# Expert rows weighted at eviction, added to x by accumulating transfers, and a last store that waits for no other

## The chip, the cores and the metric

One core of a Trainium2 chip runs one program. The number that counts is the device time in microseconds (us) of one execution, the median of several. TensorE (PE) multiplies matrices, VectorE (DVE), ScalarE (ACT) and GpSimd (POOL) work element by element. SyncE (SP) issues most transfers, on hardware queue q1; transfers issued by POOL go on software queue q0. All of them are carried out by the same 16 DMA engines.

## The reference

Two transformer blocks in float32 on 512 tokens of 1024 numbers. Only the seam between them matters here: the mixture of experts that ends the first block, and the norms behind it.

```python
def hierarchical_moe(h, ...):                 # 16 experts, 2 of them for each token
    ...                                       # combine[n, e]: the two weights of token n, else 0
    a = jnp.einsum("nd,edf->nef", hf, w_gate)
    b = jnp.einsum("nd,edf->nef", hf, w_up)
    u = jax.nn.silu(a) * b * combine.astype(hf.dtype)[..., None]
    return jnp.einsum("nef,efd->nd", u, w_down)
...
x = x + hierarchical_moe(rmsnorm(x, norm_moe_g), ...)   # end of the first block
x = rmsnorm(x, norm_final_g)
h = rms_norm(x, norm_mix_g_2); proj = h @ w_in_2        # start of the second block
```

## The kernel before

Tokens lie in four tiles of 128 rows, `k.x[:, t, :]`, 128x1024 float32 each (512 KB). Matrices are split into a high and a low part (`wh`, `wl`: ACT makes the first, DVE the second, lines 126 and 127), and a product is three matmuls (lines 112 to 114).

**Experts** (`moe`). `Route` sorts the tokens by expert into blocks of 128 slots. Every expert e fetches its rows of h from DRAM by an indirect transfer (`gather`, line 1350), multiplies them (`up`, `act`, `turn`, `down`), evicts the result from PSUM to a tile `ey` by ACT (line 1393) and puts the rows by an indirect transfer from POOL (line 1394) to the DRAM tensor `y_d`: row n for a token's first choice, row 512+n for its second, so no row is written twice. Slots without a token write nothing. Each of the 16 stores waits for the one ahead to land, because all of them write `y_d`. A loop for experts with over 128 tokens stands behind a branch (`tc.If(n > 0)`); with these inputs it is skipped.

**Seam** (`mixer2`). Instructions are written in a fixed order for PE, ACT, DVE, POOL and SP (`manual_schedule`), and every engine takes its own in that order. For each token tile t: `Combine.load` fetches the two halves of `y_d` (`yg`, SP, line 1588); `add0` and `add1` add them to x, each times a column of weights `wt` (DVE, line 1599); `gained` computes the sum of squares of x on ACT (line 1608) and z = x times the final gain on DVE (line 1609), `squares` that of z on ACT (1613); `stats` makes both norms' factors (three small DVE operations and a power on POOL, line 186); `norm` scales z (DVE, line 1628); `turn` transposes it on PE (line 218), and `lo` writes the low part (DVE, line 224). Then `k.head` multiplies with three weight tiles (`hraw`, loaded by SP, split at once by `split_w`). PE is kept busy meanwhile by `values(n)`: n of 16 steps of another product, V of the second block's cross-attention (line 608). `kv.load_v` loads its weights.

Where the loads stand on SP: the three weight tiles, the four `yg` of tiles 0 and 1, two loads for `values`, the four `yg` of tiles 2 and 3.

Of the kernel before, what the change touches and what calls it, by code (L numbers as in the profile page):

```python
# [10 lines left out]
FT = mybir.dt.float32  # L11
# [3 lines left out]
OP = mybir.AluOpType  # L15
# [1127 lines left out]
class Route:  # L1143
# [2 lines left out]

    def __init__(self, k, pool, lg, out):
        self.k, self.pool, self.lg, self.out = k, pool, lg, out  # L1150
# [59 lines left out]
    def place(self, O):  # L1210
# [33 lines left out]
        G = t(S24, "G")  # L1244
# [53 lines left out]
    def weights(self):  # L1298

        nc, t, v = self.k.nc, self.t, self.k.nc.vector  # L1300
        S4 = [P, NT, 4]
        eg = t(S4, "eg")
        v.tensor_tensor(eg, self.gl, self.gm.unsqueeze(2).to_broadcast(S4), op=OP.subtract)
        nc.scalar.activation(eg, eg, AF.Exp)
        e2 = t([P, NT], "e2")
        v.tensor_tensor(e2, self.m2, self.m1, op=OP.subtract)
        nc.scalar.activation(e2, e2, AF.Exp)
        pg = t([P, NT], "pg")
        v.tensor_reduce(pg, eg, axis=AX.X, op=OP.add)
        v.reciprocal(pg, pg)  # L1310
        wt = self.out.tile([P, 2, NT], FT, name="wt")
# [4 lines left out]
        return wt  # L1316


class Expert:
# [3 lines left out]

    def __init__(self, k, pool, hg, ids, h_d, y_d, weights):
        self.k, self.pool, self.hg, self.ids = k, pool, hg, ids
        self.h_d, self.y_d, self.weights = h_d, y_d, weights

    @staticmethod  # L1330
# [54 lines left out]
    def down(self):  # L1385
        k, nc = self.k, self.k.nc
        y = self.pool.tile([P, D], FT, name="ey")
        for c in range(2):
            w = next(self.weights)
            py = k.ps_mm.tile([P, T], FT, name="mm")  # L1390
            for i in range(2):
                k.mm3(py, self.uT[:, i, :], w[:, i, :], i == 0, i == 1)
            nc.scalar.activation(y[:, c * 512 : (c + 1) * 512], py, AF.Copy)
        nc.gpsimd.indirect_dma_start(
            out=self.y_d[:, :], out_offset=bass.IndirectOffsetOnAxis(ap=self.ids[1], axis=0),
            in_=y, in_offset=None, bounds_check=2 * T - 1, oob_is_err=False,
        )
# [9 lines left out]
        yield from Expert.down_list(k, dw[e])  # L1407


def moe(k, mst, rp, hg_pool, pools, src, w_prev, kv, vraws, early, lists):  # L1410
# [6 lines left out]
    rt = Route(k, rtp, lg, rp)  # L1417
# [77 lines left out]
    with ExitStack() as est:  # L1495
# [7 lines left out]
        with k.tc.manual_schedule(engines={*MANUAL, E.Pool}):  # L1503
            rt.choose()
            keys(3)
            rt.count()
            rt.place(ep.tile([P, D], FT, name="ey").rearrange("p (a b) -> p a b", a=8))
            keys(4)
            ids = rt.table()
            ex = [  # L1510
                Expert(
                    k, ep, hgs[e % 2], [ids[:, i, e : e + 1] for i in range(2)], h_d, y_d, weights
                )
                for e in range(NE)
            ]
            for x in ex[:2]:
                x.gather()
            xi = rt.extra()
            wt = rt.weights()
            weights.fill(2)  # L1520
            for _ in kjob:
                pass
            ex[0].rows()
            weights.fill(AHEAD)
            ex[1].rows()
            ex[2].gather()
# [17 lines left out]
        with k.tc.manual_schedule(engines={*MANUAL, E.Pool}):  # L1544
# [2 lines left out]
            kv.load_v(0, 4, vraws[0])  # L1547
            x.down()
            kv.load_v(4, 6, vraws[1])
        with k.tc.If(n > 0):  # L1550
            with k.tc.For_i(0, n) as b:
                e = nc.values_load(xi[0:1, bass.ds(b, 1)], min_val=0, max_val=NE - 1)
                idb = [ep.tile([P, 1], I32, name=f"idb{i}") for i in range(2)]
                for i in range(2):
                    nc.vector.tensor_copy(idb[i], ids[:, i, bass.ds(b + NE, 1)])
                wg, wu, wd = [w[bass.ds(e, 1)].rearrange("a r c -> (a r) c") for w in ws]
# [4 lines left out]
                x = Expert(k, ep, hgs[0], idb, h_d, y_d, weights)  # L1561
                x.gather()
                x.rows()
                for h in range(2):
# [1 line left out]
                x.act()  # L1566
                x.turn()
                x.down()
    return y_d, wt


class Combine:
# [4 lines left out]


    def __init__(self, k, pool, t):
        self.k, self.pool, self.t = k, pool, t  # L1580
        self.xs = k.x[:, t, :]

    def load(self, y_d):
        self.ys = []
        for c in range(2):
            y = self.pool.tile([P, D], FT, name="yg", bufs=2 * NT)
            r0 = c * T + self.t * P
            self.k.nc.sync.dma_start(y, y_d[r0 : r0 + P, :])
            self.ys.append(y)

    def add0(self, wt):
        self.add(0, wt)

    def add1(self, wt):
        self.add(1, wt)

    def add(self, c, wt):
        w = wt[:, c, self.t : self.t + 1]
        self.k.nc.vector.scalar_tensor_tensor(
            self.xs, self.ys[c], w, self.xs, op0=OP.mult, op1=OP.add  # L1600
        )

    def gained(self, gf):

        nc = self.k.nc
        self.hn, self.z = self.ys
# [26 lines left out]
        self.k.nc.scalar.activation(self.xs, self.z, AF.Copy, scale=self.r[:, 0:1])  # L1633


def mixer2(k, y_d, wt, kv, vraws, vdone):
# [4 lines left out]
    with ExitStack() as st:  # L1641
# [3 lines left out]
        with k.sb("m2n", bufs=1, side="right") as np_:  # L1645
# [11 lines left out]
            with k.tc.manual_schedule(engines={*MANUAL, E.Pool, E.SP}):  # L1657
# [3 lines left out]
                for g, n in ((gf, "norm_final_g"), (gm, "norm_mix_g_2")):  # L1661
                    ap = inp[n] if len(inp[n].shape) == 1 else inp[n].rearrange("a d -> (a d)")
                    nc.sync.dma_start(g, ap.partition_broadcast(P))
                hvs = []
                for c in (CQ, CK, CQ + P):
                    hvs.append(
                        k.load_raw([(None, wj[:, :, c : c + P])], KD, P, [(np_, 3)], "hraw")
                    )
                for c in cs[:2]:
                    c.load(y_d)  # L1670
                kv.load_v(6, 8, vraws[0])
                for c in cs[2:]:
                    c.load(y_d)

                def turn(t):
                    turns = k.turn_job(hT, cs[t].hn, t)
# [8 lines left out]
                    cs[t].gained(gf)  # L1685
                    cs[t].squares()

                hws = [k.split_w(v, [(np_, 3)]) for v in hvs]
                values(5)
                cs[0].add0(wt)  # L1690
                cs[0].add1(wt)
                gained(0)
                values(5)
                cs[1].add0(wt)
                cs[1].add1(wt)
                cs[0].stats()
                gained(1)
# [5 lines left out]
                cs[2].add1(wt)  # L1703
                values(2)
                lo(t0)
                cs[1].norm(gm)
                gained(2)
                values(2)
                t1 = turn(1)
                cs[3].add0(wt)  # L1710
                cs[2].stats()
                cs[3].add1(wt)
                lo(t1)
                cs[2].norm(gm)
                gained(3)
                cs[3].stats()
                cs[3].norm(gm)

# [268 lines left out]
def build(ctx, tc, inp, out):  # L1987
# [25 lines left out]
    with k.sb("m2T", bufs=1) as m2T:  # L2013
# [22 lines left out]
        with k.sb("x1kv", bufs=1) as pool:  # L2036
# [6 lines left out]
        with k.sb("moer", bufs=1) as rp:  # L2043
            kv = MemoryKV(k, k.mT2, inp["w_k_xa_2"][0], inp["w_v_xa_2"][0])
            vraws = [raws[i] for i in "pb"]
            with ExitStack() as mst:
                y_d, wt = moe(
                    k, mst, rp, lambda: (ost.close(), right(pst, "moehg", bufs=1))[1],
                    [raws[i] for i in "pqb"], oT, k.mview(inp["xa_wo"][0]), kv, vraws, early,
                    lists,  # L2050
                )
            pst.close()
            mg, gst = mixer2(k, y_d, wt, kv, vraws, bst.close)
    xst = ExitStack()

    def out2():
# [40 lines left out]
```

## Time and profile before

| | us |
|---|---|
| median of 3 runs (1672.4 to 1673.55) | 1672.48 |
| the profiled execution's own time | 1674.39 |
| its span, first to last instruction | 1672.7 |
| PE busy in the span | 1620.5 (97%) |
| DVE / ACT / POOL busy | 970.6 / 711.6 / 260.1 |

Busy times of engines overlap. The time around the span is 1.69 us. Differences are worked out in the span and then put on the median.

### The profile page before, as it was taken

What the parts mean: (1) busy time and instruction counts of PE and PEld (TensorE: products, weight loads), DVE (VectorE), ACT (ScalarE), POOL (GpSimd) and SP (SyncE); (2) the same over time, 40 slices, a digit from 0 to 9 for tenths busy, and PEclk for the clock granted to TensorE, in tenths of its full rate; (3) what the DMA queues carried; (4) which work ended last, traced back from release to release, by engine and by line L of the source; (5) the groups of instructions that cost most, each with busy time, mean ns of one, the idle gap of its engine ahead of it and who ended that gap; (6) DMA issues with size and microseconds to landing.
All of it is one profiled execution on the core that took longest, in us unless ns stands there. A gap on an engine that the chain in (4) does not pass through costs nothing.

```text
span 1672.7 us, 20550 instructions
## 1 busy us (share of the span) xinstructions
PE 1620.5 (97%) x7710; PEld 1319.2 (79%) x7710; DVE 970.6 (58%) x1494; ACT 711.6 (43%) x1136; POOL 260.1 (16%) x262
## 2 busy tenths in 40 slices
PE   7998999999999999899999999999999999999998
PEld 6866888788787886588877888888888888888886
DVE  5679997666558996748876333345545333333223
ACT  4254554344428996646644322234434222222212
POOL 3399000300012331102210011110000000000000
PEclk9999999999999999999999999999999999999999
DMA  6332323457469998742233333344123233333231
GB/s 189 90 94 65 89 82 104 161 151 227 141 197 305 316 326 293 251 124 73 67 106 102 89 94 95 95 151 126 51 76 94 75 97 89 100 89 112 90 98 53
DMA packets 253762, 218.65 MB, mean 131 GB/s; under 512 B 13871, under 2 KB 216111, under 8 KB 253660
## 3 DMA queue, kind: packets, MB, share of 16 engines
q1 hardware_dynamic: 247180, 205.51, 40.4%
q0 software_dynamic: 4608, 8.40, 1.4%
q10 hardware_dynamic: 1872, 3.41, 0.5%
q8 instruction: 61, 1.00, 0.2%
q14 instruction: 41, 0.34, 0.1%
HBM read 208.87 MB, written 16.79 MB: 135 GB/s over the span
## 4 chain that ended last, share of the span: by engine, by line
PE 70%; DVE 10%; DMA 9%; issue 6%; ACT 2%; POOL 2%; SPq 0%; POOLq 0%; DVEq 0%; ACTq 0%
PE mm L112 21%; PE mm L114 21%; PE mm L113 21%; DMA y_d<-ey,ids 7%; DVE wl L127 2%; PE mm L583 1%; DVE hn L630 1%; DVE acc L952 1%; DMA wraw<-in_w_in_dram 1%; PE s L112 1%; PE pt L209 1%; PE s L114 1%; PE s L113 1%; DMA hg<-h_d,ids 1%; PE pt L1072 1%
## 5 line engine op out<-in xcount | busy, mean ns | idle before, releaser
L127 DVE TENSOR_TENSOR wl<-wraw,wh 128x1024 fp32r<-128x1024 f32 (+1 forms) x331 | 399.7, 1221 | 362.1 <-ACT wh L126 356.1
L126 ACT ACTIVATE wh<-wraw 128x1024 fp32r<-128x1024 f32 x334 | 340.5, 1028 | 592.7 <-PE mm L113 308.9
L112 PE MATMUL mm<-hT2h,wh 128*128 128x512 f32 (+1 forms) x408 | 156.8, 384 | 0.3 <-ACT hT2h L220 0.3
L113 PE MATMUL mm<-hT2l,wh 128*128 128x512 f32 (+1 forms) x408 | 155.8, 382 | 0.3 <-DVE hT2l L224 0.3
L114 PE MATMUL mm<-hT2h,wl 128*128 128x512 f32 (+1 forms) x408 | 155.8, 382 | 0.0
L112 PE MATMUL mm<-fhTh,wh 128*128 128x512 f32 (+1 forms) x376 | 143.7, 382 | 0.0
L114 PE MATMUL mm<-fhTh,wl 128*128 128x512 f32 (+1 forms) x376 | 143.6, 382 | 0.0
L113 PE MATMUL mm<-fhTl,wh 128*128 128x512 f32 (+1 forms) x376 | 143.6, 382 | 0.0
L112 PE MATMUL mm<-hTh,wh 128*128 128x512 f32 (+1 forms) x280 | 107.9, 385 | 0.0
L113 PE MATMUL mm<-hTl,wh 128*128 128x512 f32 (+1 forms) x280 | 106.7, 381 | 0.1
L114 PE MATMUL mm<-hTh,wl 128*128 128x512 f32 (+1 forms) x280 | 106.6, 381 | 0.0
L114 PEld LDWEIGHTS mm<-hT2h,wl 128*128 128x128 f32 x408 | 76.7, 188 | 16.3
L113 PEld LDWEIGHTS mm<-hT2l,wh 128*128 128x128 f32 x408 | 76.8, 188 | 15.5 <-DVE hT2l L224 0.5
L112 PEld LDWEIGHTS mm<-hT2h,wh 128*128 128x128 f32 x408 | 76.8, 188 | 15.4 <-ACT hT2h L220 0.5
L112 PEld LDWEIGHTS mm<-fhTh,wh 128*128 128x128 f32 x376 | 70.8, 188 | 15.1
L114 PEld LDWEIGHTS mm<-fhTh,wl 128*128 128x128 f32 x376 | 70.8, 188 | 15.1
L113 PEld LDWEIGHTS mm<-fhTl,wh 128*128 128x128 f32 x376 | 70.8, 188 | 15.1
L952 DVE SCALAR_TENSOR_TENSOR acc<-cu,hw,acc 128x511 f32<-128x511 f32 (+14 forms) x90 | 71.9, 799 | 0.9
L113 PE MATMUL mm<-wl,gTh 128*128 128x512 f32 x176 | 69.6, 396 | 0.0
L114 PE MATMUL mm<-wh,gTl 128*128 128x512 f32 x176 | 69.6, 396 | 0.0
L112 PE MATMUL mm<-wh,gTh 128*128 128x512 f32 x176 | 69.6, 395 | 0.0
L1938 DVE TENSOR_TENSOR fu<-fu,mm 128x512 f32<-128x512 f32 x22 | 15.1, 688 | 82.8 <-PE mm L114 82.8
(470 smaller groups left out, 3511.0 us busy)
## 6 DMA issues: line engine op xcount, KB each, us to landing
wraw<-in_w_in_dram SPq DMA_DIRECT2D x92, 512.0 KB
wraw<-in_expert_w_gate_dram SPq DMA_DIRECT2D x64, 256.0 KB
wraw<-in_expert_w_up_dram SPq DMA_DIRECT2D x64, 256.0 KB
wraw<-in_expert_w_down_dram SPq DMA_DIRECT2D x32, 512.0 KB
wraw<-in_w_gate_ffn_dram SPq DMA_DIRECT2D x22, 512.0 KB
wraw<-in_w_up_ffn_dram SPq DMA_DIRECT2D x22, 512.0 KB
wraw<-in_w_down_ffn_dram SPq DMA_DIRECT2D x22, 512.0 KB
wraw<-in_w_out_dram SPq DMA_DIRECT2D x16, 512.0 KB
```

The lines of the kernel that those rows point to most:

```text
L112: nc.tensor.matmul(out, a.hi, b.hi, start=first, stop=False)
L113: nc.tensor.matmul(out, a.hi, b.lo, start=False, stop=False)
L114: return nc.tensor.matmul(out, a.lo, b.hi, start=False, stop=last)
L126: a = nc.scalar.activation(dst.hi, src, AF.Copy)
L127: b = (lo or nc.vector).tensor_tensor(dst.lo, src, hi, op=OP.subtract)
L209: nc.tensor.transpose(pt[:, jj, :], hn[:, half * 4 + jj :: KD], self.ident)
L583: nc.tensor.matmul(ps[:, :M], w[:, j, :], self.mT[:, j, :], start=j == 0, stop=j == KD - 1)
L630: self.k.nc.vector.scalar_tensor_tensor(self.hn[t], self.xs[t], self.r[t][:, 0:1], self.g, op0=OP.mult, op1=OP.mult)
L952: yield nc.vector.scalar_tensor_tensor(acc[:, s:], u[:, :n], w, acc[:, s:], op0=OP.mult, op1=OP.add)
L1072: nc.tensor.transpose(pt[:, kt, :], p[:, kt * P : (kt + 1) * P], k.ident)
L1938: nc.vector.tensor_tensor(u, u, pu, op=OP.mult)
```

## The change

Four parts. (1) `Route.weights` now spreads the weights over the slots (two DVE operations more), a new `row_weights` turns them into one column per expert (8 matmuls, a DVE copy), and ACT applies that column when it evicts (`scale=self.rw[:, 0:1]`). (2) In `Combine` seven of the eight loads of `y_d` become accumulating transfers on POOL's queue that add straight into x; the eighth, tile 0's second half, is loaded by SP and added by DVE without a weight. (3) The last expert's store no longer waits for the one ahead; the loads wait for both. (4) The order in `mixer2` is another one.

```diff
@@ Expert.down
-            nc.scalar.activation(y[:, c * 512 : (c + 1) * 512], py, AF.Copy)
+            nc.scalar.activation(
+                y[:, c * 512 : (c + 1) * 512], py, AF.Copy, scale=self.rw[:, 0:1]
+            )
@@ moe
+        k.tc.declare_no_dep(x.put.ins, ex[-2].put.ins, reason="no two experts put the same row")
@@ Combine
+    def load(self, c, y_d, puts, add=True):
+        k, nc = self.k, self.k.nc
+        r0 = c * T + self.t * P
+        rows = y_d[r0 : r0 + P, :]
+        if add:
+            d = nc.gpsimd.dma_start(self.xs, rows, accum_op=OP.add)
+        else:
+            d = nc.sync.dma_start(self.hn, rows)
...
-        self.k.nc.vector.scalar_tensor_tensor(
-            self.xs, self.ys[c], w, self.xs, op0=OP.mult, op1=OP.add
-        )
+    def add(self):
+        self.k.nc.vector.tensor_tensor(self.xs, self.xs, self.hn, op=OP.add)
@@ mixer2
+                cs[0].load(1, y_d, puts, False)
+                for c in cs:
+                    c.load(0, y_d, puts)
+                for c in cs[1:]:
+                    c.load(1, y_d, puts)
                 hvs = []
...
-                hws = [k.split_w(v, [(np_, 3)]) for v in hvs]
-                values(5)
-                cs[0].add0(wt)
-                cs[0].add1(wt)
+                values(9)
+                cs[0].add()
                 gained(0)
-                values(5)
-                cs[1].add0(wt)
-                cs[1].add1(wt)
-                cs[0].stats()
                 gained(1)
+                cs[0].stats()
                 cs[0].norm(gm)
-                values(2)
                 t0 = turn(0)
-                cs[2].add0(wt)
+                cs[2].gained(gf)
+                split_h()
                 cs[1].stats()
...
```

The rest of the order goes on alike: `gained`, one split, `stats`, `lo`, `squares`, three and then four steps of `values`, `norm`.

On POOL, from the last two expert stores to the first power of the seam (before, then after; what a row waits for is in brackets, by semaphore: DMASW are POOL's own transfers, DMAHW those of SP). The rows of the skipped loop are left out.

```order
L1394 DMA y_d<-ey,ids 1024x1024 [waits DMASW5_49,Activation_49]
L1394 DMA y_d<-ey,ids 1024x1024 [waits DMASW6_49,Activation_49]
...
L186 TENSOR_TENSOR r_6818<-v_6813,mhalf 128x2 [waits DVE_49]
```

```order
L1411 DMA y_d<-ey,ids 1024x1024 [waits DMASW5_49,Activation_49]
L1411 DMA y_d<-ey,ids 1024x1024 [waits Activation_49]
...
L1613 DMA x<-y_d 128x1024 [waits DMASW7_49,DMAHW6_49,DMASW6_49,DMAHW7_49,DMASW2_49,DMASW1_49]
L1613 DMA x<-y_d 128x1024 [waits DMAHW6_49]
L1613 DMA x<-y_d 128x1024 [waits DMAHW7_49]
L1613 DMA x<-y_d 128x1024
L1613 DMA x<-y_d 128x1024 [waits DMASW3_49]
L1613 DMA x<-y_d 128x1024 [waits DMASW4_49]
L1613 DMA x<-y_d 128x1024 [waits DMASW5_49,DMASW0_49]
L186 TENSOR_TENSOR r_6818<-v_6813,mhalf 128x2 [waits DVE_49]
```

The last store has lost its wait for the store ahead (DMASW6). Seven accumulating transfers stand ahead of the power: the first waits for both last stores (DMASW6, DMASW7); the fifth, sixth and seventh, the second halves of tiles 1 to 3, each wait until the first half of their tile has landed (DMASW3 to DMASW5).

On DVE, the start of the seam up to tile 1's norm (before, then after).

```order
L1599 SCALAR_TENSOR_TENSOR x<-yg,wt,x 128x1024 x2
L1609 TENSOR_TENSOR yg<-x,wraw 128x1024
L1599 SCALAR_TENSOR_TENSOR x<-yg,wt,x 128x1024 x2
L1619 TENSOR_SCALAR v_6813<-ss_6789 128x1
L1620 TENSOR_SCALAR e_6814<-v_6813 128x1
L1621 SCALAR_TENSOR_TENSOR v_6813<-ss_6789,e_6814 128x1
L1609 TENSOR_TENSOR yg<-x,wraw 128x1024
L1628 SCALAR_TENSOR_TENSOR yg<-yg,r_6818,wraw 128x1024
```

```order
L1624 TENSOR_TENSOR x<-x,yg 128x1024
L1631 TENSOR_TENSOR yg<-x,wraw 128x1024 x2
L1641 TENSOR_SCALAR v_6813<-ss_6805 128x1
L1642 TENSOR_SCALAR e_6814<-v_6813 128x1
L1643 SCALAR_TENSOR_TENSOR v_6813<-ss_6805,e_6814 128x1
L1650 SCALAR_TENSOR_TENSOR yg<-yg,r_6818,wraw 128x1024
L1631 TENSOR_TENSOR yg<-x,wraw 128x1024
L127 TENSOR_TENSOR wl<-wraw,wh 128x1024
L1641 TENSOR_SCALAR v_6840<-ss_6809 128x1
L1642 TENSOR_SCALAR e_6841<-v_6840 128x1
L1643 SCALAR_TENSOR_TENSOR v_6840<-ss_6809,e_6841 128x1
L224 TENSOR_TENSOR hT2l<-pt,hT2h 128x4x128 x2
```

The four weighted adds of tiles 0 and 1 have become one plain add. z of tile 1 (the second of the x2) now stands ahead of tile 0's statistics, so tile 0's norm comes behind whatever tile 1 waits for. A weight split (L127), which stood ahead of these rows, now stands inside.

On PE, the same seam up to the head's products (one piece of the difference; L608 are the `values`, L218 the transposes, eight for a tile).

```order
-L608 MATMUL mm<-wraw,mTh 128x512 x24
+L608 MATMUL mm<-wraw,mTh 128x512 x18
+L218 MATMUL pt<-ident,yg 128x128 x8
+L608 MATMUL mm<-wraw,mTh 128x512 x6
 L218 MATMUL pt<-ident,yg 128x128 x8
 L608 MATMUL mm<-wraw,mTh 128x512 x8
-L218 MATMUL pt<-ident,yg 128x128 x8
```

Twelve steps of `values` stood ahead of tile 0's transposes and four behind; now nine stand ahead, three between tiles 0 and 1, and four behind tile 1. (The profile has two rows for each of these matmuls.)

## Rows read from the trace of the kernel before

**Rows 1.** The page: busy time of engines, share of span, instructions.

```profile
PE 1620.5 (97%) x7710; PEld 1319.2 (79%) x7710; DVE 970.6 (58%) x1494; ACT 711.6 (43%) x1136; POOL 260.1 (16%) x262
```

**Rows 2.** Chain that ended last, 480 to 740 us: start, length, what.

```profile
618.14 47.13 DMA y_d<-ey,ids
```

**Rows 3.** PE's timeline over the seam: start, length, what, [idle before, releaser].

```profile
658.62 20.87 PE L608 MATMUL mm<-wraw,mTh 128*128 128x512 f32 x48 [0.69 <-ACT ey L1393]
685.72 1.97 PE L218 MATMUL pt<-ident,yg 128*128 128x128 f32 x8 [6.24 <-DVE yg L1628]
687.49 8.34 PE L608 MATMUL mm<-wraw,mTh 128*128 128x512 f32 x16
...
718.06 0.40 PE L112 MATMUL mm<-wh,hT2h 128*128 128x512 f32 x1
```

**Rows 4.** Windows: stretch, its length, busy time by engine (instructions), PE clock, DMA share, GB/s.

```profile
524.00:654.00 130.00, 130.00 (x634) 108.78 (x633) 123.11 (x139) 118.25 (x165) 38.43 (x25) 1.00 0.99 328
658.60:718.20 59.60, 51.64 (x241) 34.47 (x242) 34.63 (x47) 27.79 (x42) 7.16 (x6) 0.94 0.70 235
679.50:685.70 6.20, 0.00 (x0) 0.00 (x0) 5.40 (x9) 4.42 (x8) 1.64 (x1) 0.81 1.03 405
```

**Rows 5.** POOL's timeline, 640 to 735 us.

```profile
655.08 0.98 POOL L1394 DMA_INDIRECT y_d<-ey,ids  x1 [7.37 <-ACT uTh L126]
663.82 0.98 POOL L1394 DMA_INDIRECT y_d<-ey,ids  x1 [7.77 <-DMA y_d<-ey,ids]
682.71 1.64 POOL L186 TENSOR_TENSOR r<-v,mhalf 128x2 f32<-128x2 f32 x1 [17.91 <-DVE v L1621]
```

**Rows 6.** ACT's timeline: the second evictions of the last two experts.

```profile
653.94 0.60 ACT L1393 ACTIVATE ey<-mm 128x512 f32<-128x512 f32 x1 [0.78 <-PE mm L114]
...
657.97 0.60 ACT L1393 ACTIVATE ey<-mm 128x512 f32<-128x512 f32 x1 [0.80 <-PE mm L114]
```

**Rows 7.** DMA, 665 to 667 us: rate in 40 slices of 0.05 us, and queue 0.

```profile
GB/s 0 0 0 0 0 0 0 573 246 2 412 328 1 328 410 0 82 573 82 82 492 82 82 492 82 0 573 82 0 0 82 492 82 0 0 0 92 133 133 215
...
q0 software_dynamic: 144, 0.28, 38.9%
```

**Rows 8.** DMA queues, 661 to 663 us: packets, MB, share of 16 engines.

```profile
q1 hardware_dynamic: 29, 0.05, 7.4%
q0 software_dynamic: 16, 0.05, 6.6%
```

**Rows 9.** SP's timeline: the seam's first loads.

```profile
665.47 2.56 SPq L169 DMA_DIRECT2D wraw<-in_w_in_dram  x3
668.13 2.94 SPq L1588 DMA_DIRECT2D yg<-y_d  x4
```

**Rows 10.** DMA queues, 657 to 658 us.

```profile
q1 hardware_dynamic: 173, 0.33, 88.1%
q0 software_dynamic: 35, 0.06, 16.5%
```

**Rows 11.** DMA queue 1, 667 to 669 us.

```profile
q1 hardware_dynamic: 1122, 0.57, 96.7%
```

**Rows 12.** DVE's timeline: the adds of tile 1.

```profile
679.51 2.60 DVE L1599 SCALAR_TENSOR_TENSOR x<-yg,wt,x 128x1024 f32<-128x1024 f32 x2
```

**Rows 13.** Instructions that touch yg: count, duration min/median/max in ns, first and last start.

```profile
L1599 DVE SCALAR_TENSOR_TENSOR x<-yg,wt,x x8: 1276/1279/1285, 675.7 to 693.7; 128x1024 f32<-128x1024 f32 x8
L1608 ACT ACTIVATE yg<-x x4: 1056/1057/1069, 678.3 to 697.3; 128x1024 f32<-128x1024 f32 x4
L1609 DVE TENSOR_TENSOR yg<-x,wraw x4: 1215/1220/1226, 678.4 to 699.4; 128x1024 f32<-128x1024 f32 x4
...
L1633 ACT ACTIVATE x<-yg,r x4: 1135/1143/1150, 703.4 to 709.4; 128x1024 f32<-128x1024 f32 x4
```

**Rows 14.** PE's timeline at the start of the experts, 486 to 512 us.

```profile
490.57 1.86 PE L1266 MATMUL s<-B,ey 128*128 128x23 f32 x16
...
504.15 0.50 PE L112 MATMUL mm<-wh,hgTh 128*128 128x512 f32 x1 [2.11 <-ACT hgTh L126]
```

More of the change, by code (lines that the diff above doesn't have):

```diff
@@ L1143, with __init__ @@
 class Route:
-    def __init__(self, k, pool, lg, out):
-        self.k, self.pool, self.lg, self.out = k, pool, lg, out
+    def __init__(self, k, pool, lg):
+        self.k, self.pool, self.lg = k, pool, lg
         nc, t = k.nc, self.t
@@ L1243, in place @@
         S24, SS = [P, 8, NBLK + 1], [P, 8, P]
-        G = t(S24, "G")
+        self.G = G = t(S24, "G")
         v.tensor_tensor(
@@ L1310, in weights @@
         v.reciprocal(pg, pg)
-        wt = self.out.tile([P, 2, NT], FT, name="wt")
+        wt = t([P, 2, NT], "wt")
         v.tensor_scalar(wt[:, 0, :], e2, 1.0, None, op0=OP.add)
@@ L1315, in weights, with row_weights, __init__ @@
         v.tensor_tensor(wt[:, 1, :], wt[:, 0, :], e2, op=OP.mult)
-        return wt
+        self.Bw = Bw = t([P, 8, NBLK], "Bw")
+        v.tensor_tensor(Bw, self.G[:, :, :NBLK], self.G[:, :, 1:], op=OP.subtract)
+        wf = wt.rearrange("p c t -> p (c t)").unsqueeze(2).to_broadcast([P, 8, NBLK])
+        v.tensor_tensor(Bw, Bw, wf, op=OP.mult)
+    def row_weights(self):
+        k, nc = self.k, self.k.nc
+        pr = k.ps_s.tile([P, T], FT, name="s")
+        for i in range(8):
+            nc.tensor.matmul(
+                pr[:, :NBLK], self.O[:, i, :], self.Bw[:, i, :], start=i == 0, stop=i == 7
+            )
+        rw = self.t([P, NBLK], "roww")
+        nc.vector.tensor_copy(rw, pr[:, :NBLK])
+        return rw
 class Expert:
-    def __init__(self, k, pool, hg, ids, h_d, y_d, weights):
-        self.k, self.pool, self.hg, self.ids = k, pool, hg, ids
+    def __init__(self, k, pool, hg, ids, h_d, y_d, weights, rw=None):
+        self.k, self.pool, self.hg, self.ids, self.rw = k, pool, hg, ids, rw
         self.h_d, self.y_d, self.weights = h_d, y_d, weights
@@ L1392, in down @@
                 k.mm3(py, self.uT[:, i, :], w[:, i, :], i == 0, i == 1)
-            nc.scalar.activation(y[:, c * 512 : (c + 1) * 512], py, AF.Copy)
-        nc.gpsimd.indirect_dma_start(
+            nc.scalar.activation(
+                y[:, c * 512 : (c + 1) * 512], py, AF.Copy, scale=self.rw[:, 0:1]
+            )
+        self.put = nc.gpsimd.indirect_dma_start(
             out=self.y_d[:, :], out_offset=bass.IndirectOffsetOnAxis(ap=self.ids[1], axis=0),
@@ L1407, in expert_weights, with moe @@
         yield from Expert.down_list(k, dw[e])
[L1410 removed]
+def moe(k, mst, hg_pool, pools, src, w_prev, kv, vraws, early, lists):
     nc, inp = k.nc, k.inp
@@ L1416, in moe @@
     lg = rtp.tile([P, NT, 20], FT, name="lg")
-    rt = Route(k, rtp, lg, rp)
+    rt = Route(k, rtp, lg)
     raw2 = mst.enter_context(k.sb("moeraw2"))
@@ L1518, in moe @@
             xi = rt.extra()
-            wt = rt.weights()
+            rt.weights()
             weights.fill(2)
@@ L1522, in moe @@
                 pass
+            rw = rt.row_weights()
+            for e, x in enumerate(ex):
+                x.rw = rw[:, e : e + 1]
             ex[0].rows()
@@ L1555, in moe @@
                     nc.vector.tensor_copy(idb[i], ids[:, i, bass.ds(b + NE, 1)])
+                rwb = ep.tile([P, 1], FT, name="rwb")
+                nc.vector.tensor_copy(rwb, rw[:, bass.ds(b + NE, 1)])
                 wg, wu, wd = [w[bass.ds(e, 1)].rearrange("a r c -> (a r) c") for w in ws]
@@ L1560, in moe @@
                 )
-                x = Expert(k, ep, hgs[0], idb, h_d, y_d, weights)
+                x = Expert(k, ep, hgs[0], idb, h_d, y_d, weights, rwb)
                 x.gather()
@@ L1568, in moe @@
                 x.down()
-    return y_d, wt
+    return y_d, [x.put.ins.name for x in ex[-2:]]
 class Combine:
     def __init__(self, k, pool, t):
-        self.k, self.pool, self.t = k, pool, t
+        self.k, self.t = k, t
         self.xs = k.x[:, t, :]
[L1583 to L1598, printed above, removed]
-        self.k.nc.vector.scalar_tensor_tensor(
-            self.xs, self.ys[c], w, self.xs, op0=OP.mult, op1=OP.add
-        )
+        self.hn, self.z = (pool.tile([P, D], FT, name="yg", bufs=2 * NT) for _ in range(2))
+    def load(self, c, y_d, puts, add=True):
+        k, nc = self.k, self.k.nc
+        r0 = c * T + self.t * P
[4 more added lines that the diff above has]
+            d = nc.sync.dma_start(self.hn, rows)
+        for name in puts:
+            k.tc.add_manual_dep(
+                d.ins, name,
+                mybir.DependencyInfo(mybir.DependencyClass.Sync, mybir.DependencyReason.DATA),
+                reason="rows of the last experts",
+            )
+    def add(self):
+        self.k.nc.vector.tensor_tensor(self.xs, self.xs, self.hn, op=OP.add)
     def gained(self, gf):
         nc = self.k.nc
-        self.hn, self.z = self.ys
         self.ss = self.k.small.tile([P, 2], FT, name="ss2")
@@ L1633, in keep, with mixer2 @@
         self.k.nc.scalar.activation(self.xs, self.z, AF.Copy, scale=self.r[:, 0:1])
-def mixer2(k, y_d, wt, kv, vraws, vdone):
+def mixer2(k, y_d, puts, kv, vraws, vdone):
     nc, inp = k.nc, k.inp
@@ L1668, in mixer2 @@
                     )
-                for c in cs[:2]:
-                    c.load(y_d)
                 kv.load_v(6, 8, vraws[0])
-                for c in cs[2:]:
-                    c.load(y_d)
                 def turn(t):
@@ L1686, in gained, with split_h @@
                     cs[t].squares()
-                hws = [k.split_w(v, [(np_, 3)]) for v in hvs]
-                values(5)
-                cs[0].add0(wt)
-                cs[0].add1(wt)
+                hws = []
+                def split_h():
+                    hws.append(k.split_w(hvs[len(hws)], [(np_, 3)]))
+                values(9)
+                cs[0].add()
                 gained(0)
-                values(5)
-                cs[1].add0(wt)
-                cs[1].add1(wt)
+                gained(1)
                 cs[0].stats()
-                gained(1)
                 cs[0].norm(gm)
-                values(2)
                 t0 = turn(0)
-                cs[2].add0(wt)
+                cs[2].gained(gf)
+                split_h()
                 cs[1].stats()
-                cs[2].add1(wt)
-                values(2)
                 lo(t0)
+                cs[2].squares()
+                values(3)
                 cs[1].norm(gm)
-                gained(2)
-                values(2)
                 t1 = turn(1)
-                cs[3].add0(wt)
+                cs[3].gained(gf)
+                split_h()
                 cs[2].stats()
-                cs[3].add1(wt)
                 lo(t1)
+                cs[3].squares()
+                values(4)
                 cs[2].norm(gm)
-                gained(3)
+                split_h()
                 cs[3].stats()
@@ L2042, in build @@
             )
[L2043 to L2053, printed above, removed]
+        kv = MemoryKV(k, k.mT2, inp["w_k_xa_2"][0], inp["w_v_xa_2"][0])
+        vraws = [raws[i] for i in "pb"]
+        with ExitStack() as mst:
+            y_d, puts = moe(
+                k, mst, lambda: (ost.close(), right(pst, "moehg", bufs=1))[1],
+                [raws[i] for i in "pqb"], oT, k.mview(inp["xa_wo"][0]), kv, vraws, early,
+                lists,
+            )
+        pst.close()
+        mg, gst = mixer2(k, y_d, puts, kv, vraws, bst.close)
     xst = ExitStack()
```

## The prediction

> **What bounds the kernel now.** I read the busy times first: PE is busy for 97% of the span [rows 1], so nearly everything else lies beside PE, and only a place where PE waits can pay. The chain of work that ended last shows one that the change touches: it leaves PE for the stores to `y_d`, which stand in it for 47.13 us [rows 2]. PE's timeline shows what comes of that [rows 3]: the `values` run from 658.62, one wait of 6.24 us ends at 685.72 with DVE's norm of tile 0, and 718.06 is a product of the next stage. I call 685.72 T, the start of tile 0's transposes, and 718.06 the end. The windows [rows 4] give the sizes: from 658.6 to 718.2 PE works 51.64 of 59.60 us, so at most 8 us are to be had here. In the experts, 524 to 654 us, PE works 130.00 of 130.00. The granted clock was 0.81 in the idle stretch and 0.94 over the seam, 1.00 in the experts. What the seam saves or loses goes straight to the end, for PE is the bound behind it.
>
> The sum is made in the span. The profiled execution took 1674.39, 1.91 above the median of 1672.48, so I put the difference on the median. A difference under 0.2%, 3.3 us, is about what a measurement of this kernel can't tell from no change.
>
> **The last store.** Before, it is issued at 663.82, after a wait of 7.77 for the store ahead [rows 5]. Its data are there at 657.97 + 0.60 = 658.57 [rows 6]. The store ahead was issued at 655.08, 0.54 behind its own data (653.94 + 0.60); so this one goes at 659.11, 4.7 us earlier. Before, its first bytes move at 665.35 and the last near 666.9 [rows 7]: 1.5 us from issue to first byte, 1.6 us of packets. Alone it would end at 662.2. But from 661 to 663 queue 0 still carries 16 late packets and q1 29 [rows 8], and behind those of the store ahead on the same engines I let it end at 663.6. From its last byte to what waits for it is about 1.1 us, as the store ahead's packets, gone by 662.7 or so, let the next start at 663.82. The accumulating transfers start at 664.7 (ends: 663.3 if nothing holds the store, 665.1). Before, SP issues three weight tiles at 665.47 and the `yg` loads at 668.13 [rows 9]: 3.4 us won on the loads.
>
> **The accumulating transfers.** Tile 0 needs one of them and SP's plain load; tile 1 both its halves. By the order on DVE, z of tile 1 stands ahead of tile 0's statistics, so T now waits for the fifth transfer of POOL's queue (first halves of tiles 0 to 3, then tile 1's second half). The trace of before has no accumulating transfer, so its price is bounded. From below by a copy: q1 moved 0.33 MB in 88.1% of 1 us of all engines [rows 10], so a tile of 0.524 MB costs 1.40; POOL's own store, 0.28 MB in 38.9% of 2 us [rows 7], gives 1.46. From above by two copies, 2.80, since x has to be read as well as `y_d`; that store's elapsed time (0.28 MB in 1.6 us, 3.0 for a tile) lies there too. No row is nearer to one end; I take the middle, 2.1, five of them 10.5 us. In that time q1 carries one `yg` (1.40), three weight tiles in small packets, 0.524/0.57 x 1.934 = 1.78 each [rows 11], and two loads for `values` (1.40 each): 9.5 us of engine time. What share q1 takes of it is the second unknown: nothing, or 84% as at 657 us (88.1 beside 16.5, [rows 10]). With small packets (27.6 ns each by rows 11's count) against rows of 4 KB at 2.1 x 16/128 = 0.26 us, I let q1 take a quarter. Then 664.7 + 1.5 + 10.5/0.75 + 1.1 = 681.3 for the fifth landing. At 84% it would be 687.3. POOL's issues, 0.98 us each [rows 5], keep ahead of that.
>
> The row of the two queues at 657 us gave queue 0 a sixth of the engines' time. The Trainium skill ("DMA: Bandwidth & Descriptors", section "Queues, rings and completion order") says that an engine goes round the queues that have work and empties a whole packet of descriptors from one before it turns to the next; by even turns the fifth landing would be 687 too, 6 us later than I have it. No row here has both queues full, so this isn't shown.
>
> **The order behind that.** From the landing, DVE makes z of tile 1, 1.22 [rows 13]; three small operations take 0.60 (from 679.51 + 2.60 [rows 12] to the power at 682.71), the power 1.64, and from its end at 684.35 to T it is 1.37 [rows 3, 5]. Together 4.8: T = 686.1, where it was 685.72. So the earlier loads are spent on four transfers more that stand ahead of T. Nine steps of `values` are 36 rows of 0.435 (20.87/48): PE is done with them at 658.62 + 15.7 = 674.3 and idles until 686.1, 11.8 us, where it idled 6.24.
>
> Behind T, tile 1's transposes need: tile 0's transposes 1.97 and ACT's last copy of them, 0.60 as an eviction; then on ACT a square, 1.06 [rows 13], and the weight's high part, of the same form, 1.06; on DVE its low part 1.22, the small operations 0.60, the power 1.64, norm and start 1.37: 9.5 us. PE has only 1.97 and twelve rows of `values` (5.2) in that time. Behind tile 1's transposes PE is the bound again: its work behind T was 51.64 - 20.87 = 30.8, of which 1.97 and 8.34 were tile 0 and 16 rows of `values` [rows 3, 4]; the other 20.5 stay, with 16 rows at 0.435, 7.0: 27.4. So the end is T + 36.9 = 723.0, 4.9 us behind 718.06. What DVE is spared, seven weighted adds of 1.28 and 0.06 on the eighth [rows 13], stands beside waits for data and is worth nothing by itself. Equal times would need T at 681.2, the fifth landing at 676.3.
>
> **Weights at eviction.** ACT with a column of factors takes 1143 ns where it takes 1057 without [rows 13], both for 1024: 0.04 for an eviction of 512, 1.4 us for 32 of them. It hides beside PE's 130.00 of 130 while ACT is busy for 118.25 [rows 4]; only the last 0.04 is on the path. `row_weights` is 8 matmuls of 23 columns, under the 1.86 of 16 such [rows 14], and a copy of 0.2 (estimate from z's 1.22 per 1024); it lies in PE's wait of 2.11 for ACT ahead of the first expert's products. If that cover is gone it costs up to 1.9. The two new DVE operations on 184 numbers, 0.2 each by the same estimate, lie beside the two gathers. I take nothing for all of it; it makes the range's lower end worse by up to 1.9.
>
> **The sum:** the store 3.4 earlier on the loads, the transfers and z of tile 1 ahead of T +3.7, 4.6 us more behind T: +4.9, 1677.4 us.
>
> **The rivals.**
> Same: an accumulating transfer costs what a copy does. Five are 7.0 us, with the same quarter for q1 9.3; the fifth lands at 676.6, T = 681.4, the end 718.3, +0.2: 1672.7. For it: the price of POOL's own store. Against it: x must be read.
> Faster, the other side: queue 0 goes first and at the copy's price. The landing is 664.7 + 1.5 + 7.0 + 1.1 = 674.3, T = 679.1, and nothing on PE waits behind T: 1.97 + 5.2 + 27.4 = 34.6, end 713.7, -4.4: 1668.1. It decides once the fifth lands before 676.3 and tile 1's transposes within 7.2 us of T. For it: q1's small packets. Against it: the chain of 9.5 behind T.
> Slower still: each transfer reads twice, 2.80, 14.0/0.75 = 18.7 us, the fifth lands at 686.0, T = 690.8, end 727.7, +9.6: 1682.1. For it: two operands have to come. Against it: the read of x could run beside the read of `y_d`.
> The Trainium skill ("Collectives: The Full Stack", section "The bandwidth ceiling: the fold count and why AG ≠ RS ≠ AR") puts an adding transfer at two source reads on one ring, half the rate of a copy; that is this rival, and its sum is the one above. No run here shows it yet.
> That the store still waits is excluded: its row in the order has only ACT's semaphore. So is a late power on POOL, whose seventh issue goes by about 681.
>
> **How the numbers follow.** Between prices of 1.4 and 2.8, and shares of nothing and 84%, most combinations land behind 676.3. I give my forecast 0.38 (its own range 1674 to 1681), the same 0.25, faster 0.22, twice the reads or the greater share of q1 0.15. So faster by over 3.3 us 0.22, within it 0.27 (with the low end of my own case), slower 0.51. The range reaches from the faster rival, 1668, to behind the slowest, 1684.
>
> **What the profile after would show.** The last store's issue at about 659.1; POOL's first accumulating issue at 664.7; landings about 2.8 us apart; DVE's z of tile 1 waiting for a transfer until about 681; PE idle from 674.3 to 686; 9.5 us from tile 0's transposes to tile 1's. I am wrong if the landings are under 2 us apart, if z of tile 1 doesn't wait for POOL's queue, or if tile 1's transposes follow within 7.5 us. A wait of PE at 504 longer than 2.11 would price `row_weights`.

## The result

The changed kernel takes 1681.69 us (median of 5 runs, 1679.76 to 1683.76), the one before 1672.48: +9.2 us, ratio 1.0059, 95% interval 1.0046 to 1.0071. It is slower, by 0.6% and clear of the noise.

PE's timeline of the changed kernel over the seam (start, length, what, [idle before, releaser]) answers to [rows 3]:

```profile
658.03 15.72 PE L608 MATMUL mm<-wraw,mTh 128*128 128x512 f32 x36 [0.78 <-ACTq L1571]
686.81 1.94 PE L218 MATMUL pt<-ident,yg 128*128 128x128 f32 x8 [13.06 <-DVE yg L1650]
688.54 7.30 PE L608 MATMUL mm<-wraw,mTh 128*128 128x512 f32 x12
695.81 1.13 PE L218 MATMUL pt<-ident,yg 128*128 128x128 f32 x8
...
723.56 0.39 PE L112 MATMUL mm<-wh,hT2h 128*128 128x512 f32 x1
```

The one wait of 6.24 us has become one of 13.06. From the start of `values` to the end it is 723.56 - 658.03 = 65.5 us, before 718.06 - 658.62 = 59.4: +6.1. The chain of work that ended last says what PE waits for there (start, length, what):

```profile
658.25 3.69 DMA y_d<-ey,ids
662.16 0.56 issue
662.72 0.64 POOL x L1613
663.36 10.88 DMA x<-y_d
674.24 0.28 issue
674.52 8.14 DMA x<-y_d
682.78 1.23 DVE yg L1631
...
684.61 0.74 POOL r L186
685.37 1.30 DVE yg L1650
686.67 0.14 issue
686.81 1.94 PE pt L218 x8
```

Read it downwards: the last store; POOL's issues; tile 1's first half, landed at 674.24; its second half, issued only then and landed at 682.66; z of tile 1, and only then tile 0's norm. Nineteen microseconds pass in two accumulating transfers, from issue to landing, with what stands ahead of them in the queue. The windows answer to [rows 4] (stretch, its length, busy PE, PEld, DVE, ACT, POOL, clock, DMA share, GB/s):

```profile
673.80:686.80 13.00, 0.00 (x0) 0.03 (x1) 3.24 (x7) 3.63 (x8) 3.27 (x4) 0.70 1.08 220
686.80:703.20 16.40, 16.39 (x43) 8.40 (x44) 9.72 (x16) 8.91 (x15) 1.39 (x2) 0.83 0.39 131
```

While PE stood idle the granted clock fell, to 0.70 in the mean, and behind T, where PE works without a gap, it is still 0.83: tile 0's transposes take 1.94 and tile 1's 1.13. All DMA engines are busy in the idle stretch (1.08), and yet they move 220 GB/s; in the idle stretch of before it was 405. The two queues in it, 671 to 673 us (packets, MB, share of 16 engines):

```profile
q0 software_dynamic: 103, 0.39, 96.3%
q1 hardware_dynamic: 102, 0.05, 12.6%
```

A tile of 0.524 MB costs 0.524/0.39 x 0.963 x 2 = 2.6 us of all engines.

### The profile page after: what moved, and what is told of

Same layout as the page of the kernel before. It is cut to its first block, busy times and chain, and to the rows that moved or that the text cites. A ratio compares the mean times of both kernels' runs of the same rounds, so it can differ in the third digit from the quotient of the medians.

```text
span 1679.9 us, 20587 instructions
## 1 busy us (share of the span) xinstructions
PE 1624.9 (97%) x7726; PEld 1322.1 (79%) x7726; DVE 963.2 (57%) x1490; ACT 714.0 (42%) x1136; POOL 254.2 (15%) x269
## 4 chain that ended last, share of the span: by engine, by line
PE 84%; DVE 9%; ACT 2%; DMA 2%; issue 2%; POOL 1%; SPq 0%; POOLq 0%; ACTq 0%; DVEq 0%
PE mm L112 24%; PE mm L113 24%; PE mm L114 24%; DVE wl L127 2%; PE mm L583 2%; PE pt L209 2%; DMA x<-y_d 1%; DVE hn L630 1%; DVE acc L952 1%; PE pt L1072 1%; PE s L112 1%; PE mm L608 1%; PE s L113 1%; PE s L114 1%; PE mm L120 1%
## 5 line engine op out<-in xcount | busy, mean ns | idle before, releaser
L127 DVE TENSOR_TENSOR wl<-wraw,wh 128x1024 fp32r<-128x1024 f32 (+1 forms) x331 | 400.9, 1222 | 356.5 <-ACT wh L126 351.5
L114 PEld LDWEIGHTS mm<-hTh,wl 128*128 128x128 f32 x280 | 54.3, 194 | 10.9
```

The source lines that it names most:

```text
L114: return nc.tensor.matmul(out, a.lo, b.hi, start=False, stop=last)
L127: b = (lo or nc.vector).tensor_tensor(dst.lo, src, hi, op=OP.subtract)
```

## The experiments

All are compared with runs of the kernel before on the same chip (medians 1671.94 to 1672.16); e1 to e4, e5 and e6, e7 to e10, and e11 ran on different chips, so between these groups the ratios tell more than the medians. "Seam" is from the first row of `values` to the first product `mm<-wh,hT2h`, "behind" from there to the first product `mm<-wh,mg2h`, both in the profiled execution.

| | median us | ratio, 95% interval | T behind `values` | seam | behind |
|---|---|---|---|---|---|
| before | 1672.48 | | 27.1 | 59.4 | 403.6 |
| changed | 1681.69 | 1.0046 to 1.0071 | 28.8 | 65.5 | 405.5 |
| e1 plain loads, SP | 1673.41 | 0.9998 to 1.0016 | 21.4 | 57.8 | 405.9 |
| e2 plain loads, POOL | 1676.63 | 1.0013 to 1.0031 | 24.5 | 61.0 | 406.0 |
| e3 tile by tile | 1683.49 | 1.0058 to 1.0085 | 26.3 | 68.2 | 405.5 |
| e4 store waits again | 1683.68 | 1.0051 to 1.0078 | 32.1 | 68.7 | 405.5 |
| e5 before, store freed | 1669.20 | 0.9979 to 0.9997 | 24.7 | 56.4 | 403.5 |
| e6 before, weights moved | 1673.44 | 1.0004 to 1.0021 | 26.2 | 58.4 | 405.4 |
| e7 changed, pool kept | 1678.68 | 1.0028 to 1.0055 | 28.9 | 65.3 | 403.9 |
| e8 weights and store | 1669.44 | 0.9971 to 0.9990 | 24.9 | 56.3 | 403.6 |
| e9 issues behind | 1682.41 | 1.0053 to 1.0080 | 20.3 | 64.5 | 405.5 |
| e10 first new order | 1672.26 | 0.9996 to 1.0014 | 19.0 | 58.7 | 403.6 |
| e11 second new order | 1666.09 | 0.9947 to 0.9973 | 17.9 | other order | |

**e1, eight plain loads on SP.**

```diff
-            d = nc.gpsimd.dma_start(self.xs, rows, accum_op=OP.add)
+            d = nc.sync.dma_start((self.z, self.hn)[c], rows)
...
+        for y in (self.z, self.hn):
+            self.k.nc.vector.tensor_tensor(self.xs, self.xs, y, op=OP.add)
```

> The changed kernel, but all eight loads of y_d are plain, on SP's queue in the same order, and DVE adds them without weights (eight adds of 1.22 us). Theory (the price of the accumulating transfers, 2.6 us a tile as queue 0's rows of the changed kernel show, sets T): six plain loads at 1.40 land by about 673, the adds and norms of tiles 0 and 1 follow, T near 680 where the changed kernel has 686.81, the end 7 to 9 us earlier than its 723.56, so 2 to 3.7 us under the kernel before. Rival (the order of the seam costs it, whatever carries the rows): T stays at 685 or later and the time within 2 us of the changed kernel.

T fell by 7.4 us against `values`, and the seam by 7.7. In these rows T stands at 678.46, tile 1's transposes again 9.0 behind it:

```profile
678.46 1.97 PE L218 MATMUL pt<-ident,yg 128*128 128x128 f32 x8 [5.67 <-DVE yg L1649]
680.22 6.87 PE L608 MATMUL mm<-wraw,mTh 128*128 128x512 f32 x12
687.43 1.13 PE L218 MATMUL pt<-ident,yg 128*128 128x128 f32 x8 [0.34 <-DVE yg L1649]
```

So in the same order, the way the rows are carried is worth 7.7 us of the seam. The median, though, was expected below the kernel before and isn't: 2.3 us are lost behind the seam (405.9 beside 403.6; see e7).

**e2, the same seven on POOL's queue, without adding** (`nc.gpsimd.dma_start((self.z, self.hn)[c], rows)`).

> As the run with eight plain loads, but the seven transfers stay on POOL's queue, without accumulating, and DVE adds. It tells the accumulation from the queue. If accumulating is what costs 2.6 us a tile, seven plain ones take 1.4 to 1.6 us of all engines each, the fifth lands by 675, T near 681 and the end within 2 us of the run on SP's queue. Rival (the queue of POOL is the slow part): 2.5 us or more a tile here too, T at 686 or later.

Both causes are real. Queue 0 from 671 to 673 us, now with plain transfers:

```profile
q0 software_dynamic: 190, 0.70, 88.6%
q1 hardware_dynamic: 188, 0.09, 15.9%
```

A tile costs 0.524/0.70 x 0.886 x 2 = 1.33 us: adding doubles the price. But T is 3.1 us later than in e1, against the theory, and the median 3.2 us over e1's. Two things are seen, and no run parts them. The first packets come 2.3 us behind the first issue (663.68 to 666.0), in e1 1.0 (662.30 to 663.3). And the weight tiles, which in e1 stand behind the eight loads in the same queue, run beside them here, as from 668 to 669 us:

```profile
q1 hardware_dynamic: 372, 0.19, 62.6%
q0 software_dynamic: 39, 0.13, 37.0%
```

The changed kernel is 5.1 us above e2 by the medians, 4.5 in the seam; that is the adding. The adding kernel also lets three second halves wait for first halves, but queue 0 hardly ran dry by it: from 668 to 682 us it is busy for 87% or more of every microsecond but one (58.0% from 678 to 679), an estimated 0.4 us of the 4.5.

**e3, tile by tile, and e9, the same with the last two transfers issued later.**

```diff
 cs[0].add(); gained(0)
-gained(1)
 cs[0].stats(); cs[0].norm(gm); t0 = turn(0)
+split_h(); lo(t0); values(3); gained(1)
...
```

```diff
 cs[0].stats()
+for c in cs[2:]:
+    c.load(1, y_d, puts)
 cs[0].norm(gm)
```

> The changed kernel with its accumulating transfers, but the order behind values(9) goes tile by tile: add, z, squares, statistics and norm of tile 0 before anything of tile 1, and so on. Theory (T waits for the fifth transfer only because z of tile 1 stands ahead of tile 0's statistics): tile 0 needs what has landed by 671.5, T falls from 686.81 to about 677, PE's idle of 13 us ahead of T to 3, tile 1's transposes come at about 687, and the end is 714 to 717, 7 to 9 us under the changed kernel and 1 to 4 under the one before. Rival (the sum of the transfers bounds the seam, so the idle only moves behind tile 0): PE idles as long between tiles 0 and 1 as is won ahead of T, and the time stays within 2 us of the changed kernel.

> The tile-by-tile order with accumulating transfers once more, but the sixth and the seventh transfer are issued behind tile 0's power on POOL. In the tile-by-tile run that power started at 680.52, right behind the seventh issue, though its input was there at 675.04. Theory (POOL's queue of issues held it): the power comes at about 675.5, T falls from 682.94 to 677.5 to 678.5, and the time by 3 to 6 us against the tile-by-tile run. Rival (something else held tile 0): T within 1.5 us of 682.94.

POOL's timeline, e3, then e9:

```profile
679.96 0.85 POOL L1613 DMA_DIRECT2D x<-y_d  x1 [2.14 <-DMA x<-y_d]
680.52 1.05 POOL L186 TENSOR_TENSOR r<-v,mhalf 128x2 f32<-128x2 f32 x1
```

```profile
675.14 0.73 POOL L186 TENSOR_TENSOR r<-v,mhalf 128x2 f32<-128x2 f32 x1 [0.17 <-DVE v L1643]
676.98 0.89 POOL L1613 DMA_DIRECT2D x<-y_d  x1 [1.11 <-DMA x<-y_d]
```

In e3 the power stands behind an issue that waits for a transfer, and POOL takes its instructions in order. In e9 it runs at 675.14 and T comes at 677.25, as its theory had it, 20.3 us behind `values` and 8.5 sooner than in the changed kernel. Yet e9's seam is only 1.0 us shorter and its median no lower. So e9's theory held for T and failed for the time; on the time e3's rival was right for both runs. Its reason, the sum of the transfers, is not what ends last in e9, though. There PE idles 3.92 us ahead of tile 1's transposes, at 689.16. The second half of tile 1 is there at 682.28, when ACT squares x, but on DVE z of tile 1 stands behind the first weight split and tile 0's `lo`, and that split waited, through ACT, for a weight tile that was 18.27 us on its way beside the accumulating transfers (the chain, then ACT, then DVE):

```profile
662.47 18.27 DMA wraw<-in_w_in_dram
682.28 1.06 ACT L1630 ACTIVATE yg<-x 128x1024 f32<-128x1024 f32 x1 [0.41 <-DMA x<-y_d]
681.90 1.23 DVE L127 TENSOR_TENSOR wl<-wraw,wh 128x1024 fp32r<-128x1024 f32 x1 [4.71 <-ACT wh L126]
683.04 1.28 DVE L224 TENSOR_TENSOR hT2l<-pt,hT2h 128x512 fp32r<-128x512 f32 x2
684.24 1.22 DVE L1631 TENSOR_TENSOR yg<-x,wraw 128x1024 f32<-128x1024 f32 x1
```

T alone isn't worth its time; what stands between tile 0 and tile 1 counts as much. With z ahead of the split some 2 us more could have been won (an estimate, 684.24 - 682.28), which wasn't tried; the seam would still be longer than before, about 62.5 beside 59.4.

**e4, the last store waits again** (the line with `declare_no_dep` taken out).

> The changed kernel, but the last expert's store waits for the one ahead again. Theory (T hangs on the transfers, and these on the store): the last store is issued 4 to 5 us later and everything to the end with it, 3.5 to 5 us over the changed kernel. Rival (the two stores share the engines, so a store issued early lands little earlier): under 1.5 us over the changed kernel.

T is 3.3 us later behind `values`, the seam 3.2 longer: a little under the theory's 3.5 to 5 and well over the rival's 1.5. The median stands 2.0 over the changed kernel's, measured in another set of runs.

**e5, the freed store alone in the kernel before**, and **e6, the weights alone** (`row_weights`, the factor at eviction, plain adds).

> The kernel before, with nothing but the last store freed of its wait (the loads wait for both last stores). Theory: the loads of the seam start 4 to 5 us earlier, the weight splits and adds on DVE with them, PE's wait of 6.24 us at T shrinks to 1 to 2, and the time falls by 4 to 6 us. Rival (T of the kernel before is set by DVE's own work, or the store lands no earlier): under 1.5 us.

> The kernel before, with nothing but the weights moved: row_weights, the factor at eviction, and plain adds on DVE. Theory: the 8 matmuls of row_weights stand in PE's stream ahead of the experts (1.7 us, as in the changed kernel), but keep PE at work there, and the granted clock, 0.5 for 3.4 us at 504 us in the kernel before, stays up, so that by the experts' end nothing is lost: within 1 us of the kernel before. Rival: the 1.7 us are lost to the end, 1.5 to 2 us slower.

e5: the seam is 3.0 us shorter and the median 2.7 lower, half of what was hoped. PE's wait ahead of T is still 3.83, since DVE's splits and adds follow the loads as before. e6: 1.5 slower, the rival's size, but not by its mechanism: e6's 1.8 us lie behind the seam, not ahead of it. On the clock the theory is borne out in part. From 500 to 515 us the granted clock (the third number from the end) is 1.00 in all nine profiles of kernels with `row_weights`; of the four without, it is 0.89 in before, e10 and e11 and 1.00 in e5. Here before, e10, e5 and e6:

```profile
500.00:515.00 15.00, 11.72 (x53) 9.55 (x52) 7.57 (x8) 8.37 (x12) 1.98 (x2) 0.89 0.90 286
500.00:515.00 15.00, 11.84 (x52) 9.58 (x52) 8.22 (x10) 9.67 (x13) 1.98 (x2) 0.89 0.88 286
500.00:515.00 15.00, 12.65 (x63) 10.51 (x64) 11.32 (x14) 12.78 (x18) 3.43 (x3) 1.00 0.98 318
500.00:515.00 15.00, 13.50 (x76) 11.38 (x75) 7.83 (x10) 8.77 (x12) 2.10 (x2) 1.00 0.91 300
```

No gain of it shows where the experts end: `values` start at 656.6 to 658.3 us with `row_weights` and at 654.2 to 658.7 without.

**e7, the changed kernel with the small tile of weights in its own pool**, which leaves the tiles behind it at their old addresses:

```diff
-        wt = t([P, 2, NT], "wt")
+        wt = self.out.tile([P, 2, NT], FT, name="wt")
```

> The changed kernel, but the small tile of weights lies in a pool of its own again, as before, so that the tiles allocated behind it get their old addresses. In every kernel with the weights at eviction, PE takes 1.8 us longer from 725 to 1100 us (matmuls on the tile hT2 230 to 235 ns where they took 229 to 233), in those without it none. Theory (the place of the tiles in SBUF): those 1.8 us are gone, and the time is 1 to 2.5 us under the changed kernel; the seam stays as it is. Rival (the weights themselves, or chance): no difference.

The stretch behind falls from 405.5 to 403.9 us, the seam stays at 65.3. The median is 3.0 us under the changed kernel's, on another chip; the rows show 1.6 of it. Two groups of instructions from 725 to 1100 us (count | busy us, mean ns | idle), the changed kernel, then e7:

```profile
L113 PE MATMUL mm<-wl,hT2h 128*128 128x512 f32 x62 | 24.7, 399 | 0.0
L112 PE MATMUL mm<-wh,hT2h 128*128 128x512 f32 x62 | 24.6, 397 | 0.0
```

```profile
L112 PE MATMUL mm<-wh,hT2h 128*128 128x512 f32 x60 | 23.7, 394 | 0.0
L113 PE MATMUL mm<-wl,hT2h 128*128 128x512 f32 x60 | 23.5, 392 | 0.0
```

The same products take 3 to 7 ns more each, with no wait. That is some 0.6 us; the three larger groups (`mm<-hT2h,wh` and the two like it), some 335 products each, have means of 398, 396 and 396 ns against 397, 394 and 395, some 1.3 us more. Which tile's address does it wasn't tried.

**e8, weights and store, plain loads, the order of before, the pool kept.**

> The weights at eviction and the freed store alone, with plain loads on SP and the order of the kernel before (weight splits first, then tile by tile), and the small pool kept. It tells the order from the transfers. If the new order costs something of its own, this beats the run with eight plain loads in the new order by 2 to 4 us in the seam (655 to 725 us), so 1668 to 1670; if the order is neutral, the seam takes the same as there, and the time is 1671 to 1672.

Its seam is 1.5 us shorter than e1's: the new order, of SP's loads and of the instructions, costs that, more than nothing and less than the 2 to 4 expected. With the pool kept, moving the weights costs nothing that shows (1669.44 beside e5's 1669.20).

**e10 and e11, versions to beat both.** From e5; the loads of tiles 0 and 1 ahead of the weight tiles, and another order; in e11 also another place for the splits and the last transposes (from e10 to e11, in part):

```diff
-                cs[1].stats()
-                split_h()
-                cs[1].norm(gm)
+                cs[1].stats()
+                cs[1].norm(gm)
+                lo(t0)
+                values(2)
+                split_h()
...
-                ps0 = k.head(hws, hT, {(0, 0): turn2, (0, 1): lambda: lo(turn(3))})
+                ps0 = k.head(hws, hT, {(0, 1): turn2, (0, 2): lambda: lo(turn(3))})
```

> A version that should beat both: the kernel before with the freed store alone, the loads of tiles 0 and 1 ahead of the weight tiles on SP, and an order in which tiles 0 and 1 are normed before the first weight split, ten steps of values ahead of tile 0's transposes and two ahead of tile 1's. By the rows of the run with the freed store alone, tile 0's rows land 5 to 6 us earlier, T at about 18 us behind the start of values instead of 24.7, and PE hardly waits: 4 to 7 us under that run, 1662 to 1666. Rival (the weight tiles, landing later, hold the splits): 1668 or more.

> The second try at a version that beats both: the freed store and the loads of tiles 0 and 1 ahead of the weight tiles as in the first try, but tile 1's norm ahead of the first weight split on DVE, the splits spread behind it, and the transposes of tiles 2 and 3 one third of the head later. In the first try the split held tile 1's norm from 677.5 to 680.28, and PE waited 4.49 us for tile 3's transposes, with 12.5 us of products behind them. Theory (these two places cost it): T about 19 us behind the start of values, PE's waits together under 4 us, 1664 to 1667. Rival (DVE has more to do in the seam than PE leaves time for, in any order): 1669 or more.

e10 failed, at the rival's time: T came 19.0 behind `values`, but the first split held tile 1's norm, and PE waited 4.49 us for tile 3. It wasn't the weight tile's landing that held the split, as the rival had it: ACT made the split's high part at 678.04, straight behind its copies of tile 0's transposes, without a wait for a transfer. e11 mends both. PE's transposes and `values` in it:

```profile
658.66 17.43 PE L608 MATMUL mm<-wraw,mTh 128*128 128x512 f32 x40 [0.69 <-ACT ey L1393]
676.59 1.16 PE L218 MATMUL pt<-ident,yg 128*128 128x128 f32 x8 [0.50 <-DVE v L1626]
677.59 3.60 PE L608 MATMUL mm<-wraw,mTh 128*128 128x512 f32 x8
681.02 1.05 PE L218 MATMUL pt<-ident,yg 128*128 128x128 f32 x8
681.91 7.03 PE L608 MATMUL mm<-wraw,mTh 128*128 128x512 f32 x16
```

The wait ahead of T is 0.50 us, and the granted clock is 1.00 over the seam. 1666.09 us, ratio 0.9947 to 0.9973: 5.9 us under the kernel before, without a single accumulating transfer. Of these, 2.7 are the freed store's (e5), the rest is the loads' place and the order together.

## Why the prediction was right, and where its terms were off

The time lies in the range and on the side that was forecast, 4.3 us above the point. The mechanism stands: T waits for the fifth transfer, and PE pays. T was put at 686.1 and came at 686.81, but out of terms that were off in both directions, which is luck: against the forecast the transfers started 2.0 us sooner, their first packets came 2.9 later, the five landings took 0.5 longer (from about 667.1 to 682.66), and the way from the last of them to T was 0.65 shorter.

- **The last store.** Its issue was forecast for 659.11; it came at 658.25, the experts having ended 0.6 sooner. The packets still under way did not hold it: landed at 661.94, where 663.6 + 1.1 was forecast. The transfers were issued at 662.72, 2 us earlier than thought: 5.4 us won on the loads (668.13 before) and not 3.4. At the end the freed store is worth 3.0 in e5 and 3.2 in e4.
- **From issue to first byte**, 1.5 us was taken from one store. It was the worst term: the first issue is at 662.72, and from 665 to 667 us the profile has no row for queue 0, only q1; queue 0 begins between 667.0 and 667.2, at least 4.3 us behind. The engines weren't full meanwhile, and in e2 it was 2.3 us; what makes the difference stays open. From 665 to 667, then from 667 to 667.2 us:

```profile
q1 hardware_dynamic: 703, 0.36, 68.7%
```

```profile
q1 hardware_dynamic: 63, 0.03, 56.6%
q0 software_dynamic: 2, 0.01, 30.0%
```

- **The price.** The middle, 2.1, was wrong. It is 2.6, near the upper bound, and 1.33 without adding (e2). The Trainium skill ("Collectives: The Full Stack", section "The bandwidth ceiling: the fold count and why AG ≠ RS ≠ AR") says of the reduction in a collective that adding needs two source reads and halves the rate; these traces agree for an accumulating load, at a factor of 2.6/1.33 = 2.0.
- **The share of q1**, a quarter, was too large: 12.6% beside 96.3%. The counts tell why: 103 and 102 packets, one for one. A packet of queue 0 has 0.39 MB/103, 3.8 KB, one of q1 0.5 KB. The Trainium skill ("DMA: Bandwidth & Descriptors", section "Queues, rings and completion order") has engines go round the queues and drain a whole packet of several descriptors from one before the next. The equal counts fit even turns, though the rows, whose packets are about one line of 4 KB or 0.5 KB each, don't show how many make a turn. Even turns in packets were far from even turns in time, as the prediction had read them. Price and share offset each other: 2.1/0.75 = 2.8 us apart was forecast, and POOL's issues of the second halves, each at a landing, came at 674.52, 677.36 and 680.34, 2.8 and 3.0 apart.
- **From landing to T** 4.8 was forecast, 682.66 to 686.81 is 4.15: the power took 0.74, not 1.64. **Behind T** 36.9 was forecast and 36.75 measured; PE worked through it at a lower clock, where the prediction had a wait of 2.3 for tile 1. The chain behind that wait was there: tile 1's transposes came 9.0 behind tile 0's, in e1 and e2 too, where PE did wait for them (0.34 and 1.01). That slower products filled just this gap is luck.
- **The weights** at nothing: right for the operations themselves (e8 beside e5), wrong for the kernel as changed. The removed pool moved other tiles, and 405.5 - 403.6 = 1.9 us were lost behind the seam. No step of the prediction looked there. The wait that was to price `row_weights`, 2.11 at 504 us, was 1.54 in the changed kernel.

In the profiled executions the change is 1679.9 - 1672.7 = 7.2 us: 6.1 in the seam, 1.9 behind it, 0.6 won ahead of it, where executions differ by more than that, and 0.2 won behind `mm<-wh,mg2h`. The other 2 of the 9.2 are the 1.91 by which the profiled execution of before stood above its median. By part, from the medians or, where it says so, from the rows: the freed store -2.7 (e5), the weights nothing with the pool kept (e8), the moved addresses 1.9 (rows), the order 1.5 (e8 to e1, rows), POOL's queue 3.2 (e1 to e2), the adding 5.1 (e2 to the changed kernel): together 9.0. These kernels form a chain from before to changed, so a sum near the whole was to be expected; single parts are less sure (the intervals reach some 1.5 us either way, and e8 to e1 is 4.0 by the medians, 3.4 in these parts).

Of the rivals, the one with two reads gave the price, and its time, 1682.1, came nearest, but by luck: its T was 4.0 us too late and its seam 3.5 us too long (+9.6 beside +6.1). The 1.9 behind the seam and the 1.91 by which the profiled execution of before stood above its median, neither of them in its sum, made up for that.

## What to carry to other kernels

An accumulating transfer takes an add from an engine that had time and puts its double price on the path: before using it, look whether the engine that adds is the one waited for. Here it wasn't, and the transfers were. Count what stands ahead of the first consumer in each queue, transfers and POOL's issues alike; a transfer that waits on POOL holds POOL's arithmetic. When the critical wait is for loads, free the store ahead of them (2.7 us here), and move the loads and the order around them (some 3 us more) first. Moving the loads alone isn't enough: whatever stands between two tiles on DVE, a weight split in e9 and e10, takes the gain away.

## What the hardware showed that was not expected

- Plain transfers of the same rows cost 3.2 us more on POOL's queue than on SP's, though a tile costs 1.33 us there. The queue's first packets came 2.3 us behind the issue (1.0 on SP's), 4.3 with accumulating transfers, and the weight tiles ran beside them.
- With both queues full, packets came in equal numbers (103 and 102, 190 and 188), so a queue of 0.5 KB packets got 12.6% and 15.9% of the engines' time.
- The place of tiles in SBUF alone changed PE's products by 1 to 7 ns of 395, 1.6 to 1.9 us over 404.
